# Gate's and up's products of a step issued chunk by chunk in turn instead of one whole product after the other

## The chip, the core and the metric

The kernel runs on one NeuronCore of a Trainium2 chip. The metric is the device time of one execution in microseconds (us). Three runs of the kernel before took 1248.95, 1249.93 and 1252.76 us; the median is 1249.93 us.

## What is computed

One block of a hybrid streaming encoder, for 1024 tokens of 1024 channels in float32: a Mamba-2 group and a stick-breaking attention group side by side, `out_proj`, and then the part that matters here, a SwiGLU channel mixer with 2816 hidden channels (`D_FF`):

```python
h = rms_norm(x, pre_ffn_gain[layer])
f = (jax.nn.silu(h @ w_gate[layer]) * (h @ w_up[layer])) @ w_down[layer]
x = x + rms_norm(f, post_ffn_gain[layer])
```

The changed code makes `h @ w_gate` and `h @ w_up`.

## The kernel before, in words

**How gate and up are tiled.** Gate and up are each made as the seven products of Winograd's form of Strassen's product. A quad `p` (0 to 10) is a pair of tiles of 128 hidden channels; the tokens are two blocks of 512, the 1024 input channels two halves. A *product* is [128 channels of f] x [512 tokens] summed over 512 input channels, so four chunks `k` of 128. Every operand is held as a high and a low part (`split`, lines 70 to 73: ScalarE makes the high part, VectorE the low part), and a chunk is three matmuls (`mm3`, lines 75 to 78: high x high, high x low, low x high). So a product is 12 matmuls of 128x128 by 128x512 into one PSUM bank (`product`, lines 887 to 891), all behind each other. Each matmul has its own load of weights (the left operand); the right operand is streamed.

**A step.** `quad(p, "g")` and `quad(p, "u")` (lines 896 to 928) are generators that give one product at each `next`. `step(p)` (lines 986 to 994) takes gate's next product and then up's: 12 matmuls of gate, 12 of up. Seven steps make a quad. Each of gate and up has four banks: `a` (products 0 and 1, with the right operands `B11` and `B21`), `b` (product 2, `T2`), `c` (products 3 and 5, `T3` and `T4`), `e` (products 4 and 6, `T1` and `B22`). The eight banks are taken from a ring of eight, so a bank comes back with the next quad. Product 1 adds to what product 0 left in bank `a`, and ScalarE copies bank `a` to `p1` between them (line 903); products 5 and 6 add to banks that VectorE read one step or more before.

**The left operands.** `left_gen` (lines 933 to 975) makes them, gate's and up's in turn; `pump(1 + LOOK)` ahead of each step keeps five steps' worth of pairs. There are ten pairs of places (`flhi`, `fllo`; tiles named `fhi`/`flo` in the pool `fw`), so a new pair waits until the step that used its place has been multiplied. The first two steps of quad 0 take theirs from `early_ops` (lines 1013 to 1022) instead, tiles `eo` in the pool `fwA`.

**Where the operands lie.** The pool `fw` is on the right side of SBUF, and so is `wo` (the operands of out_proj). `fwA` and `rpA`, `rpB` (the right operands `B11`, `B21`, `T2`, `T3` and `T1`, `T4`, `B22`) are on the left side. In out_proj (`out_mm`, lines 790 to 801) a bank gets 24 matmuls behind each other; the right operand is in `wo`, the left one (`yhl`) in `wo` too, but for positions 2 and 3, whose `yhl` takes the place of `T3` in `rpA` (line 764). The down product (`mms`, lines 1275 to 1280, and its loop from line 1286) has both operands on the right side, and gives three matmuls to each of four banks in turn.

**What sets the order.** The framework's planner orders the instructions of each engine before the run: in its own reckoning of time it takes, for an engine that is free, the earliest traced instruction whose inputs it reckons ready. The order in the program is the priority, not the order itself. On the chip each engine then runs its list in order.

**Round the change.** The first step of quad 0 stands before the products of out_proj's last position (line 1098), the second behind them (1116), quad 1's first two at lines 1124 and 1128 round `out_tail(7)`, which makes the last columns of `T2` and `T3`. From line 1230 on a loop goes through the rest: pump, step, gate (`gate`, lines 996 to 1004, makes a block of silu(gate) x up and stores it).

Of the kernel before, what the change touches and what calls it, by code (L numbers as in the profile page):

```python
# [13 lines left out]
PSUM = bass.MemoryType.PSUM  # L14
DRAM = bass.MemoryType.DRAM

P = 128
S = 1024
# [16 lines left out]
# what in_proj makes, in order; "ssd" from where on SSD's steps run beside the tiles  # L35
PLAN = ('qkv1', 'x0', 'x1', 'x2', 'x3', 'x4', 'x5', 'qkv2', 'x7', 'x6', 'ssd', 'qkv3', 'z0', 'z1', 'r0', 'z2', 'z3', 'wo', 'l1', 'o0')
# how far attention is where the other stream is 0, 1/8, .. 1 done
# [10 lines left out]
def tile_hybrid_block(  # L48
# [15 lines left out]
    """The rows of x and out run backwards in time (row s is token S-1-s), so that every  # L64
    running product over earlier tokens is a forward scan along the free axis."""
# [4 lines left out]
    def split(hi, lo, src):  # L70
        """hi + lo == src, hi and lo each exact in float32r."""
        A.copy(hi, src)  # L72
        V.tensor_tensor(lo, src, f32(hi), ALU.subtract)  # L73
# [6 lines left out]
    # ------------------------------------------------------------------ constants  # L80
# [20 lines left out]
    # TensorE's clock rises with use: products of ones while the first loads run  # L101
# [3 lines left out]
    # tri[s, l] = 1 where s >= l  # L105
    tri = const.tile([P, P], F32, name="tri")
    G.affine_select(tri, ones_f, [[-1, P]], ALU.is_ge, 0.0, base=0, channel_multiplier=1)
    # scan floor: 1 where the key is not strictly before the query, 0 elsewhere
# [3 lines left out]
    # column h is 1 on the 64 partitions of head h of a pair  # L112
# [11 lines left out]
    # DRAM scratch  # L124
# [5 lines left out]
    # means of squares and what they make 1 / rms: even heads, odd heads, SSD groups  # L130
# [8 lines left out]
    # ------------------------------------------------------------------ right side: x * gain and in_proj weights  # L139
# [4 lines left out]
    # the rows' 1 / rms scales columns here, so it is applied to what comes out of in_proj  # L144
# [13 lines left out]
    # sel16 sums the products of the two halves of w2  # L158
# [11 lines left out]
    # columns of w_in in the order of their use; each tile is loaded and split while the one before it  # L170
    # is multiplied
# [5 lines left out]
    def fetch_w(half=None):  # L177
        """The next column tile, or one half of it."""
        if cols:
            name, col = cols[0]  # L180
            w = w_tiles.setdefault(name, [])
            for dh in range(2) if half is None else (half,):
                w.append(load_w_half(col, name, dh))
            if len(w) == 2:
                cols.pop(0)
# [8 lines left out]
    # ------------------------------------------------------------------ pre-mix norm, first products  # L194
# [40 lines left out]
    # ------------------------------------------------------------------ left side: attention, conv and SSD work  # L235
# [20 lines left out]
    def qkv_tiles(j, st):  # L256
        """What takes q, k (each in its two parts) and v of a pair of heads out of PSUM, to DRAM."""
# [38 lines left out]
    # ------------------------------------------------------------------ dt, decays  # L296
    def dt_stage():
# [18 lines left out]
        # softplus(x) = max(x, 0) + log1p(exp(-|x|)), log1p(e) = 2 atanh(e / (2 + e))  # L316
# [43 lines left out]
        # attention's sigmoids, which need these, wait for the last exponential: ScalarE changes its table once  # L360
# [4 lines left out]
    # ------------------------------------------------------------------ conv tiles  # L365
# [38 lines left out]
    # ------------------------------------------------------------------ SSD  # L404
# [76 lines left out]
    def mean_sq(src, sel, rows, n, cnt, ps=None, start=True, stop=True):  # L481
        """Means of squares over channels, to the rows of ss_d."""
# [32 lines left out]
    # ------------------------------------------------------------------ stick-breaking attention  # L515
    CH = {128: [128], 256: [256], 384: [384], 512: [512], 640: [384, 256], 768: [512, 256], 896: [512, 384], 1024: [512, 512]}

    def prep_head(j, st, h):
        """Keys over both halves of the partitions, the query's high part beside its low part."""
# [29 lines left out]
    def weigh(head, qb):  # L549
        """A key k weighs sigmoid(z_k) * prod_{q < i < k} sigmoid(-z_i)."""  # L550
# [20 lines left out]
    def turn(ws, g, jj):  # L571
        """Weights of 256 queries and 256 keys, keys to the partitions, split."""
# [27 lines left out]
    def attention(st):  # L600
        """All heads, as one stream of small steps: products with the values lag the transposes,
        the next queries' weights run ahead of them."""
# [53 lines left out]
    def merge(ga, gb):  # L656
        """Interleave attention with the other stream, as PACE has it."""
# [47 lines left out]
    # ------------------------------------------------------------------ out_proj: the products  # L705
    # position p of a block of 128 tokens: from here on the last rows come first
# [14 lines left out]
    # the channels in the order of their use: attention's first, the SSD's second group last  # L721
    KO = (4, 5, 6, 7, 0, 1, 2, 3)

    def fetch_wo():
        """W_out's rows in the order of their use, and the places of their two parts."""
# [31 lines left out]
    def out_load(p, part):  # L757
        """A block of the mixed channels, scaled by their 1 / rms, split: all but the SSD's second
        group, that group, or all."""
# [89 lines left out]
    # ------------------------------------------------------------------ out_proj, post-mix norm, residual, pre-ffn norm  # L849
    # positions 0 .. 7 of a block of 128 tokens: from here on the last rows come first  # L850
# [3 lines left out]
    def row_rstd(ssq):  # L854
        """-2 (ssq / D + eps) ** -0.5 for [P, 2] partial sums; the gains it multiplies take in the -1 / 2."""
# [15 lines left out]
    # Gate and up as the seven products of Winograd's form of Strassen's product: blocks of 512  # L871
    # tokens, halves of d, and pairs of tiles of f. h2 is the right operand:
    #   [b11 b12; b21 b22], halves of d by halves of the tokens
# [13 lines left out]
    def product(ps, lop, rop, start):  # L887
        """ps = or += the product; a bank that was read goes on accumulating after that."""
        (ah, al), (bh, bl) = lop, rop
        for k in range(4):  # L890
            mm3(ps, ah[:, k, :], al[:, k, :], bh[:, k, :], bl[:, k, :], start and k == 0, k == 3, not start)

    gp = fw = None
    lops = []

    def quad(p, name):
        """The 2 x 2 blocks of W^T h from seven products. c11 is left in PSUM."""
# [3 lines left out]
        product(a, lops[x], B11, True)  # L901
# [3 lines left out]
        product(a, lops[x], B21, False)  # L905
        yield a
        b = bank("pb" + name)
        product(b, lops[x], T2, True)
# [4 lines left out]
        product(c, lops[x], T3, True)  # L913
# [4 lines left out]
        product(e, lops[x], T1, True)  # L918
        V.tensor_tensor(u3, e, u3, ALU.add)
        yield u3  # L920
        product(c, lops[x], T4, False)
# [3 lines left out]
        product(e, lops[x], B22, False)  # L925
# [7 lines left out]
    def left_gen():  # L933
        """The left operands in the order of their use, gate and up in turn."""
# [51 lines left out]
    def step(p):  # L986
        """The next product of gate's and of up's quad p."""
        if p not in quads:
            quads[p], done[p] = (quad(p, "g"), quad(p, "u")), 0
        cg, cu = [next(q) for q in quads[p]]  # L990
# [5 lines left out]
    def gate(t):  # L996
        """A block of a from gate's and up's."""
# [8 lines left out]
    # which block of a the products make  # L1006
    where = {1: (0, 0), 4: (1, 1), 5: (1, 0), 6: (0, 1)}

    with es_o:
# [3 lines left out]
        def early_ops():  # L1013
            """The left operands of the first two products."""
# [35 lines left out]
        def out_tail(sb, t):  # L1050
# [20 lines left out]
            # T3 = b22 - b12, T2 = T3 + b11, T1 = b12 - b11, T4 = b21 - T2: its product enters with that sign  # L1071
# [50 lines left out]
        # not the ring's next banks: those hold what waits for the last norm  # L1122
# [7 lines left out]
    # ------------------------------------------------------------------ gate and up  # L1130
# [241 lines left out]
```

## Time and profile before

| | |
|---|---|
| median of three runs | 1249.93 us |
| span of the profiled execution | 1249.6 us |
| TensorE busy (share of the span) | 1204.2 us (96%) |
| VectorE busy | 932.1 us (75%) |
| ScalarE busy | 587.7 us (47%) |
| mean granted TensorE clock | 0.989 |

The profile gives one execution. Its instruction rows cover the span, 1249.6 us from the first to the last instruction; the median of the separate runs is 0.3 us above it. A line such as `L76 PE MATMUL pag<-B11h,flhi` is line 76 of the kernel on TensorE: the product that writes gate's bank `a` (`pag`; `pau` is up's) from the right operand `B11`'s high part and the left operand's high part. PEld is the load of weights. `pd` are the down product's banks, `po` out_proj's. Matmuls overlap, so it is the distance from start to start that tells their pace, not the duration of one.

### The profile page before, as it was taken

What the parts mean: (1) busy time and instruction counts of PE and PEld (TensorE: products, weight loads), DVE (VectorE), ACT (ScalarE), POOL (GpSimd) and SP (SyncE); (2) the same over time, 40 slices, a digit from 0 to 9 for tenths busy, and PEclk for the clock granted to TensorE, in tenths of its full rate; (3) what the DMA queues carried; (4) which work ended last, traced back from release to release, by engine and by line L of the source; (5) the groups of instructions that cost most, each with busy time, mean ns of one, the idle gap of its engine ahead of it and who ended that gap; (6) DMA issues with size and microseconds to landing.
All of it is one profiled execution on the core that took longest, in us unless ns stands there. A gap on an engine that the chain in (4) does not pass through costs nothing.

```text
span 1249.6 us, 16320 instructions
## 1 busy us (share of the span) xinstructions
PE 1204.2 (96%) x5641; PEld 972.0 (78%) x5641; DVE 932.1 (75%) x1461; ACT 587.7 (47%) x1115; POOL 92.1 (7%) x232
## 2 busy tenths in 40 slices
PE   8998999999999998998799999999999999999997
PEld 7776778787887776787678888888888888888885
DVE  7478988778997887676897565566555558998777
ACT  7347655556655666444653332333233325444543
POOL 0041110010110100011200000000000000000000
PEclk9998999999999999999899999999999999999999
DMA  5693252445466326754872212312132198133336
GB/s 188 194 358 107 67 152 82 142 117 178 142 181 190 118 93 212 228 173 159 271 207 93 93 60 93 101 59 93 52 100 98 58 327 318 62 124 101 102 135 235
DMA packets 139882, 183.23 MB, mean 147 GB/s; under 512 B 10660, under 2 KB 94852, under 8 KB 139800
## 3 DMA queue, kind: packets, MB, share of 16 engines
q1 hardware_dynamic: 128544, 151.18, 38.3%
q0 software_dynamic: 7424, 25.17, 5.5%
q10 hardware_dynamic: 3832, 5.84, 1.3%
q8 instruction: 44, 0.72, 0.2%
q14 instruction: 38, 0.31, 0.1%
HBM read 132.23 MB, written 49.92 MB: 146 GB/s over the span
## 4 chain that ended last, share of the span: by engine, by line
PE 69%; DVE 14%; DMA 8%; issue 4%; ACT 4%; SPq 2%; DVEq 0%; ACTq 0%
PE pd L77 5%; PE pd L76 5%; PE pd L78 5%; DVE sn L567 3%; DMA Rb<-r_d 3%; PE o L590 2%; PE tp L578 2%; PE pj_x L76 2%; PE pj_x L78 2%; PE pcg L76 2%; PE pj_x L77 2%; PE pcu L76 2%; PE peg L76 2%; PE peu L76 2%; PE peu L77 2%
## 5 line engine op out<-in xcount | busy, mean ns | idle before, releaser
L72 ACT CAST flhi<-fraw 128x512 fp32r<-128x512 f32 x102 | 62.7, 622 | 174.1 <-PE pcg L77 37.0
L77 PE MATMUL pd<-folo,fohi 128*128 128x512 f32 x260 | 101.2, 389 | 0.0
L76 PE MATMUL pd<-fohi 128*128 128x512 f32 x260 | 101.2, 389 | 0.0
L78 PE MATMUL pd<-fohi,folo 128*128 128x512 f32 x260 | 101.1, 389 | 0.0
L567 DVE TENSOR_TENSOR_SCAN sn<-sn,smask 128x1024 f32<-128x1024 f32 (+3 forms) x64 | 87.4, 1366 | 17.7 <-ACT sn L563 17.7
L73 DVE TENSOR_TENSOR fllo<-fraw,flhi 128x512 fp32r<-128x512 f32 x102 | 69.6, 686 | 38.9 <-ACT flhi L72 38.5
L72 ACT CAST fohi<-rt 128x512 fp32r<-128x512 f32 x83 | 48.9, 618 | 51.2 <-PE pd L77 30.7
L563 ACT ACTIVATE sn<-zp,msc 128x512 f32<-128x512 f32 (+2 forms) x96 | 56.0, 585 | 34.3 <-PE zp L562 30.6
L582 ACT CAST wh<-tp 128x512 fp32r<-128x512 f32 (+1 forms) x80 | 42.7, 545 | 38.4 <-PE tp L578 37.9
L72 ACT CAST flhi<-fs 128x512 fp32r<-128x512 f32 x44 | 27.2, 622 | 70.4 <-PE peg L77 37.0
L73 DVE TENSOR_TENSOR folo<-rt,fohi 128x512 fp32r<-128x512 f32 x83 | 55.2, 694 | 6.4 <-ACT fohi L72 6.4
L583 DVE TENSOR_TENSOR wl<-tp,wh 128x512 fp32r<-128x512 f32 (+1 forms) x80 | 49.7, 628 | 10.8 <-ACT wh L582 10.3
L564 ACT ACTIVATE sp<-zp,msc 128x512 f32<-128x512 f32 (+2 forms) x96 | 55.8, 584 | 2.5 <-PE tp L578 2.5
L76 PEld LDWEIGHTS pd<-fohi 128*128 128x128 f32 x260 | 48.8, 188 | 10.3
L78 PEld LDWEIGHTS pd<-fohi,folo 128*128 128x128 f32 x260 | 48.8, 188 | 10.1
L77 PEld LDWEIGHTS pd<-folo,fohi 128*128 128x128 f32 x260 | 48.8, 188 | 10.1
L1004 POOL DMA_DIRECT2D a_d<-sg x44 | 23.7, 540 | 392.4 <-DVE sg L1003 392.4
L76 PE MATMUL pj_x<-hh,wh_x 128*128 128x512 f32 x128 | 52.5, 410 | 0.0
L578 PE MATMUL tp<-ident,sp 128*128 128x128 f32 x288 | 47.6, 276 | 5.0 <-DVE sp L568 4.5
L76 PE MATMUL po<-woh,yhl 128*128 128x512 f32 x128 | 51.0, 399 | 1.0 <-ACT yhl L72 1.0
L78 PE MATMUL po<-woh,yhl 128*128 128x512 f32 x128 | 51.0, 400 | 0.6 <-DVE yhl L73 0.5
L78 PE MATMUL pj_x<-hh,wl_x 128*128 128x512 f32 x128 | 51.1, 399 | 0.0
(422 smaller groups left out, 3479.4 us busy)
## 6 DMA issues: line engine op xcount, KB each, us to landing
ps<-a_d SPq DMA_DIRECT2D x55, 256.0 KB
fraw<-in_w_gate_dram SPq DMA_DIRECT2D x22, 512.0 KB
fraw<-in_w_up_dram SPq DMA_DIRECT2D x22, 512.0 KB
a_d<-sg POOLq DMA_DIRECT2D x44, 256.0 KB, 2.5
rt<-in_w_down_dram SPq DMA_DIRECT2D x33, 256.0 KB
rt<-a_d SPq DMA_DIRECT2D x22, 256.0 KB
ps<-in_w_down_dram SPq DMA_DIRECT2D x22, 256.0 KB
xt<-in_x_t_dram SPq DMA_DIRECT2D x8, 512.0 KB
```

What stands on the lines that cost most here:

```text
L72: A.copy(hi, src)
L73: V.tensor_tensor(lo, src, f32(hi), ALU.subtract)
L76: T.matmul(ps, lhsT=ah, rhs=bh, start=start, stop=False, skip_group_check=more)
L77: T.matmul(ps, lhsT=ah, rhs=bl, start=False, stop=False, skip_group_check=more)
L78: T.matmul(ps, lhsT=al, rhs=bh, start=False, stop=stop, skip_group_check=more)
L563: A.activation(sn[:, 1 + off : 1 + off + cw_], zp[:, 0:cw_], AF.Sigmoid, scale=rqn[:, qb : qb + 1])
L564: A.activation(sp[:, off : off + cw_], zp[:, 0:cw_], AF.Sigmoid, scale=rqp[:, qb : qb + 1])
L567: V.tensor_tensor_scan(sn[:, 1 : 1 + W], sn[:, 1 : 1 + W], smask[:, 0:W], 1.0, ALU.mult, ALU.max)
L578: T.transpose(tp[:, P * i : P * i + P], ws[a][:, co : co + P], ident)
L582: A.copy(wh[:, 0:n_], tp[:, 0:n_])
L583: V.tensor_tensor(wl[:, 0:n_], tp[:, 0:n_], f32(wh[:, 0:n_]), ALU.subtract)
L590: T.matmul(o[:, 0:cw_], lhsT=vv[:, k, h, :], rhs=wt[:, c0 : c0 + cw_], start=(first and k == kb + 1 and wt is wh), stop=(last and k == kb ...
```

## The change

`product` becomes a generator that stops after each of its first three chunks. `step` takes one chunk of gate's and one of up's in turn, until both are through. So a step is issued as 3 matmuls of gate, 3 of up, 3 of gate and so on; each product's evacuation stands directly behind its own last chunk, gate's ahead of up's last chunk. The matmuls, their operands, banks and flags are the same, and so are all other instructions. The rest of the diff takes out comments and docstrings.

```diff
     def product(ps, lop, rop, start):
         (ah, al), (bh, bl) = lop, rop
         for k in range(4):
             mm3(ps, ah[:, k, :], al[:, k, :], bh[:, k, :], bl[:, k, :], start and k == 0, k == 3, not start)
+            if k < 3:
+                yield MORE
 
     gp = fw = None
+    MORE = "more"
     lops = []
 
     def quad(p, name):
...
         a = bank("pa" + name)
-        product(a, lops[x], B11, True)
+        yield from product(a, lops[x], B11, True)
         p1 = e_tile(2 * x + p % 2, "p1" + name)
         A.copy(p1, a)
         yield
-        product(a, lops[x], B21, False)
+        yield from product(a, lops[x], B21, False)
         yield a
...
     def step(p):
         if p not in quads:
             quads[p], done[p] = (quad(p, "g"), quad(p, "u")), 0
-        cg, cu = [next(q) for q in quads[p]]
+        got = [MORE, MORE]
+        while any(g is MORE for g in got):
+            got = [next(q) if g is MORE else g for q, g in zip(quads[p], got)]
+        cg, cu = got
         del lops[:2]
```

The other five products of a quad are changed in the same way as the two shown.

## Rows read from the trace of the kernel before

**Rows 1.** The profile's page: busy time of each engine over the span; the granted TensorE clock in 40 slices of the span (tenths of full speed).

```profile
PE 1204.2 (96%) x5641; PEld 972.0 (78%) x5641; DVE 932.1 (75%) x1461; ACT 587.7 (47%) x1115; POOL 92.1 (7%) x232
...
PEclk9998999999999999999899999999999999999999
```

**Rows 2.** The chain of work that ended last, in order of time, round 639 us: start us, length us, what.

```profile
638.37 0.61 DVE u3g L915
...
639.12 0.47 PE pcg L76
```

**Rows 3.** Two stretches, gate's and up's stream from the chain's turn to TensorE on, and the down product: the stretch, its length, then busy us and instructions of each engine, the granted clock, the DMA share and GB/s.

```profile
639.12:1031.19 392.07, 392.07 (x1681) 315.45 (x1681) 238.81 (x374) 123.58 (x205) 22.12 (x41) 1.00 0.31 103
1031.19:1240.90 209.71, 209.55 (x924) 173.16 (x923) 180.65 (x308) 99.20 (x196) 0.54 (x1) 1.00 0.44 153
```

**Rows 4.** TensorE's matmuls in order of time, steps 0 and 1 of a quad in the middle of the stream: start us, duration us, line, out<-in.

```profile
795.99 0.40 PE L76 MATMUL pag<-B11h,flhi 128*128 128x512 f32 x1
...
798.32 0.40 PE L77 MATMUL pag<-B11l,flhi 128*128 128x512 f32 x1
798.56 0.39 PE L78 MATMUL pag<-B11h,fllo 128*128 128x512 f32 x1
798.79 0.40 PE L76 MATMUL pau<-B11h,flhi 128*128 128x512 f32 x1
...
801.59 0.40 PE L76 MATMUL pag<-B21h,flhi 128*128 128x512 f32 x1
```

**Rows 5.** The loads of weights at the same place.

```profile
798.56 0.19 PEld L76 LDWEIGHTS pau<-B11h,flhi 128*128 128x128 f32 x1
798.79 0.19 PEld L77 LDWEIGHTS pau<-B11l,flhi 128*128 128x128 f32 x1
```

**Rows 6.** Matmuls of the down product: 12 of them from the first row to the last.

```profile
1120.28 0.39 PE L76 MATMUL pd<-fohi 128*128 128x512 f32 x1
...
1123.00 0.39 PE L76 MATMUL pd<-doh 128*128 128x512 f32 x1
```

**Rows 7.** Matmuls of out_proj's position 6 (its `yhl` in `wo`), the 7th and the 22nd of the 24 that go to its first bank.

```profile
560.02 0.39 PE L76 MATMUL po<-woh,yhl 128*128 128x512 f32 x1
...
563.42 0.39 PE L76 MATMUL po<-woh,yhl 128*128 128x512 f32 x1
```

**Rows 8.** Matmuls of out_proj's position 3 (its `yhl` in `rpA`), the 4th and the 24th of the 24 that go to its first bank.

```profile
523.20 0.40 PE L76 MATMUL po<-woh,yhl 128*128 128x512 f32 x1
...
527.85 0.39 PE L78 MATMUL po<-woh,yhl 128*128 128x512 f32 x1
```

**Rows 9.** Matmuls of gate and up with the same right operands' pool: up's product 1 of quad 0, its first and last, with the left operand `eo`; then gate's product 0 of quad 1, its 2nd and 11th, with the left operand `fl`.

```profile
595.87 0.39 PE L76 MATMUL pau<-B21h,eo 128*128 128x512 f32 x1
...
598.37 0.39 PE L78 MATMUL pau<-B21h,eo 128*128 128x512 f32 x1
...
599.70 0.39 PE L77 MATMUL pag<-B11l,flhi 128*128 128x512 f32 x1
...
601.79 0.39 PE L77 MATMUL pag<-B11l,flhi 128*128 128x512 f32 x1
```

**Rows 10.** ScalarE at the place of rows 4: start us, duration us, line, out<-in, and idle time before with what ended it.

```profile
798.81 0.62 ACT L72 CAST flhi<-fraw 128x512 fp32r<-128x512 f32 x1 [2.18 <-PE pag L77]
799.34 0.58 ACT L903 COPY p1g<-pag 128x512 f32<-128x512 f32 x1
```

**Rows 11.** The instructions of the tile `pag`: the copy between products 0 and 1, with its count and its least, median and greatest duration (ns).

```profile
L903 ACT COPY p1g<-pag x11: 568/580/587, 583.5 to 995.3; 128x512 f32<-128x512 f32 x11
```

**Rows 12.** TensorE in quad 0, at the starts of steps 2 and 5.

```profile
617.84 0.50 PE L76 MATMUL pbg<-T2h,flhi 128*128 128x512 f32 x1 [3.26 <-ACT T2h L72]
619.07 0.79 PE L76 MATMUL pbu<-T2h,flhi 128*128 128x512 f32 x1 [0.72 <-ACT flhi L72]
619.66 0.63 PE L77 MATMUL pbg<-T2l,flhi 128*128 128x512 f32 x1
...
638.24 0.40 PE L78 MATMUL peu<-T1h,fllo 128*128 128x512 f32 x1
639.12 0.47 PE L76 MATMUL pcg<-T4h,flhi 128*128 128x512 f32 x1 [0.48 <-DVE u3g L915]
...
639.89 0.39 PE L76 MATMUL pcg<-T4h,flhi 128*128 128x512 f32 x1
```

**Rows 13.** ScalarE's cast that ends the wait at 617.84 us; VectorE's two reads of the banks `c` in quad 0.

```profile
617.20 0.59 ACT L72 CAST T2h<-pt 128x512 fp32r<-128x512 f32 x1 [1.66 <-DVE pt L1077]
...
638.29 0.69 DVE L915 TENSOR_TENSOR u3g<-pcg,p1g 128x512 f32<-128x512 f32 x1
...
639.49 0.69 DVE L915 TENSOR_TENSOR u3u<-pcu,p1u 128x512 f32<-128x512 f32 x1
```

**Rows 14.** The first step of quad 0: TensorE's first matmuls, and ScalarE's cast and VectorE's subtraction that make up's left operand.

```profile
574.33 0.77 PE L76 MATMUL pag<-B11h,eo 128*128 128x512 f32 x1 [3.75 <-DVE tm L1039]
574.89 0.63 PE L77 MATMUL pag<-B11l,eo 128*128 128x512 f32 x1
...
575.74 0.63 PE L76 MATMUL pag<-B11h,eo 128*128 128x512 f32 x1
...
576.80 0.60 ACT L72 CAST eo<-er 128x512 fp32r<-128x512 f32 x1
...
577.43 0.69 DVE L73 TENSOR_TENSOR eo<-er,eo 128x512 fp32r<-128x512 f32 x1 [0.35 <-ACT eo L72]
```

More of the change, by code (lines that the diff above doesn't have):

```diff
@@ L904, in quad @@
         yield
-        product(a, lops[x], B21, False)
+        yield from product(a, lops[x], B21, False)
         yield a
         b = bank("pb" + name)
-        product(b, lops[x], T2, True)
+        yield from product(b, lops[x], T2, True)
         V.tensor_tensor(p1, b, p1, ALU.add)
@@ L912, in quad @@
         c = bank("pc" + name)
-        product(c, lops[x], T3, True)
+        yield from product(c, lops[x], T3, True)
         u3 = e_tile(4 + x, "u3" + name)
@@ L917, in quad @@
         e = bank("pe" + name)
-        product(e, lops[x], T1, True)
+        yield from product(e, lops[x], T1, True)
         V.tensor_tensor(u3, e, u3, ALU.add)
         yield u3
-        product(c, lops[x], T4, False)
+        yield from product(c, lops[x], T4, False)
         c21 = tmp()
@@ L924, in quad @@
         yield c21
-        product(e, lops[x], B22, False)
+        yield from product(e, lops[x], B22, False)
         c12 = tmp()
```

## The prediction

> **What bounds the kernel now.** I read the page first: TensorE is busy 96% of the span, at the full granted clock but for two slices [rows 1]. But matmuls overlap, so a busy TensorE can still be issuing slower than it could. Next the chain of work that ended last: until 639 us other engines are on it, and with VectorE's read of gate's bank `c` it turns to TensorE [rows 2]. From there to the down product TensorE is busy without a break [rows 3]. So whatever the change does to TensorE's stream between 639 and 1031 us reaches the end one to one; what it does ahead of that has idle time to fall into.
>
> Next the pace. In gate's and up's stream 1680 matmuls take 392.07 us, 233.4 ns from start to start (the row counts 1681, one of them cut by the border). In the down product 924 take 209.71 us, 227.0 ns, and 12 of them without any disturbance 2.72 us, 226.7 ns [rows 3, 6]. The difference, 6.7 ns a matmul, is what the change could be after: 1680 x 6.7 = 11.2 us, 0.9%.
>
> **Is it the bank?** Two things differ between the streams: how often the bank changes (every 12 matmuls, every 3) and where the operands lie. The trace has cases that separate them.
> - Out_proj's position 6 gives 24 matmuls to one bank. From the 7th to the 22nd they take 3.40 us, 15 distances of 226.7 ns [rows 7]: the fast pace with the longest stay in a bank.
> - Position 3 runs the same lines with the same stay. Only its left operand lies in `rpA`, on the left, and its right one on the right: 20 distances take 4.65 us, 232.5 ns [rows 8].
> - Up's product 1 of quad 0 is the code that is changed, 12 matmuls in one bank. Its left operand `eo` and its right one `B21` both lie on the left: 11 distances in 2.50 us, 227.3 ns. Gate's product 0 a few us later has its left operand in `fw`, on the right: 9 distances in 2.09 us, 232.2 ns [rows 9].
> - The down product has both on the right, and is fast [rows 6].
>
> So 24, 12 and 3 matmuls to a bank all run at 227 ns where both operands are on one side, and 24 and 12 both at 232 to 233 where they are on two. The change of bank itself leaves no mark: `pag` to `pau` is 0.23 us like the distances beside it [rows 4]. The loads agree. Each load of weights starts with the matmul before it and lasts 0.19 us, and the next matmul starts 0.04 us behind its end [rows 4, 5]: a loop of load and matmul, with no bank in it. The change moves no operand. What the trace lacks is the fourth case, operands on two sides and a bank change every three: it is between 0 and -11.2 us, and I take 0, since three rows of four speak for the place and none for the bank.
>
> **The change part by part.**
> *Count.* No instruction is added or removed: 24 matmuls and 24 loads a step as before, the same casts, copies, DMAs. Generators cost nothing on the chip. No queue is moved past another.
>
> *The hand-over from product 0 to product 1* is what gets worse. Both use bank `a`, and ScalarE must have copied it in between. Now up's 12 matmuls (2.8 us) lie between gate's last one and its next into that bank; the copy takes 0.58 us [rows 11] and is hidden. Afterwards only three matmuls of up's lie there. Gate's last one starts at 798.56; its next would start 4 x 0.233 us later, at 799.49. But ScalarE first takes the cast for the pair that has just come free, and starts the copy at 799.34, to 799.92 [rows 10]; a matmul starts 0.05 us after the cast that it waits for (617.20 + 0.59 to 617.84) [rows 12, 13], so 799.97. That is 0.48 us of wait, and a stream that has stopped loses another 0.07 us (639.12 to 639.89 are three distances in 0.77 us instead of 0.70) [rows 12]: 0.55 us. If ScalarE takes up's cast ahead of up's copy as well, at its 0.53 us from start to start [rows 10], that copy ends at 800.98, and up's first matmul, due 0.77 us behind gate's, waits 0.29 + 0.07 us more: 0.9 us. Queued behind the wait is all of TensorE's stream. It comes once a quad; quad 0 has out_proj's last position in between, quad 1 has idle TensorE behind it (3.26 us [rows 12]), so it counts for quads 2 to 10: 9 x 0.55 = 5.0 us, 9 x 0.9 = 8.2 us at most.
>
> What can hide it is the planner. Where it reckons an input late, it takes the next matmul that is ready: at 619.07 it has put up's first matmul between gate's first and second, since gate's second needs `T2`'s low part [rows 12]. Product 2 needs neither bank `a` nor a new operand, so its first chunk can go into the gap; two matmuls are 0.47 us. Then nothing is lost but the rest of a matmul and perhaps the restart. Ends: 0 and 0.9 us a quad. I take 0.15 us (the 0.07 of the restart and a third of a matmul), as this planner has filled such a gap in this very stage: 9 x 0.15 = 1.4 us.
>
> The Trainium skill speaks against the change here: Perfetto Trace Analysis, Optimizing Tensor Performance, Matmuls, says that independent groups should rotate through banks so that the evacuation of one overlaps the next group's matmuls. The change rotates faster but leaves the evacuation of bank `a` less to overlap with; by that rule alone the unfilled price above holds. The copy that is hidden now agrees with it.
>
> *The other banks.* `c` is read between products 3 and 5, `e` between 4 and 6, with a step of 5.6 us (795.99 to 801.59 [rows 4]) between: nothing. Evacuations now come in pairs at a step's end, instead of 2.8 us apart; VectorE is busy 238.81 of 392.07 us [rows 3], and the next reader is a step away: nothing. One place is tight, quad 0's step 5. Gate's product waits there until 639.12 for VectorE; up's bank `c` is read from 639.49 to 640.18, and 0.14 us later (as for gate's) a matmul can start, at 640.32. Up's product comes a whole product behind gate's now; interleaved it is due at 639.89 [rows 12, 13]: 0.43 us, or 0 if gate's next chunk goes ahead. I take 0.2.
>
> *The places of left operands* come free for gate at the end of a step instead of its middle. They are refilled four steps ahead, 22 us: nothing.
>
> *Quad 0's first step.* Up's left operand is cast until 577.40 and has its low part at 578.12. It is needed behind gate's 12 matmuls now; interleaved, behind three, at 575.74 [rows 14]. Unfilled that is 1.7 us; gate's own chunks can fill it, and TensorE idles 3.26 us before 617.84 in any case [rows 12]. I take 0, and 1.7 as the end.
>
> *The pace after a stop.* With operands on two sides the pace has been 232.2 to 232.5 ns [rows 8, 9] and 233.4 [rows 3]; it went from the one to the other at the stop of 639 us. If new stops draw it anew, up to 1680 x 1.0 = 1.7 us come back. I take 0.
>
> Sum: 1.4 + 0.2 = 1.6 us on a span of 1249.6, 1251.2; the median of the runs is 0.3 above the span, so **1251.5 us**. Its own range is 1248 (pace 1.7 better, all filled) to 1254.5 (0.3 us a quad, 1.7 at the start).
>
> **The rivals.**
> *The bank sets the pace when the operands are on two sides.* For: the down product changes bank every three and is the fast one. Against: rows 7 to 9. Price 11.2 us: 1251.5 - 11.2 = 1240.3 us. 10%. A pace between the two: 1246, 2%.
>
> *The hand-over stays open.* The planner reckons the copy done in time, so it leaves the order as traced, and the chip waits once a quad. Place: the first matmul of product 1, quads 2 to 10. Price 5.0 us with 0.43 us at step 5 and some of the start: 1255.5; 8.2 us: 1259. It decides from 0.4 us a quad on (9 x 0.4 = 3.6 us). For: ScalarE's cast goes ahead of the copy now [rows 10]. Against: the filling at 619.07. 25%.
>
> *The clock falls.* If TensorE's short stops at each hand-over took the granted clock from 2.4 to 1.2 GHz, matmuls would start some 0.425 us apart as at 574.89 to 575.74 [rows 14], behind an idle 3.75 us; 12 such a quad cost 12 x 0.19 x 9 = 21 us: 1272. Against: the stop of 0.48 us at 639.12 left the pace at 0.23 us [rows 12], and the down product with its bank changes runs at a granted clock of 1.00 [rows 3]. 2%. The Trainium skill (TensorE: Matmul & The Clock Gate, A second HAM failure mode: psum-queue depth-cycling) tells of a kernel whose cycling through banks left such small gaps that the clock went up and down; by that page this rival would be likelier, but the down product's row is against it.
>
> *The change doesn't do what it says*: the planner puts whole products back behind each other. It takes them by the order of the program where all is ready, so only here and there: 3%, 1250.
>
> **How the numbers follow.** The forecast has 58%. This kernel's measurement tells 0.3% from no change, 3.75 us, so 1246.2 to 1253.7. Faster: the bank and the pace between, 12%. Slower: the open hand-over 25, the clock 2, and 4 of the forecast's 58: 31%. The same: 54 and the 3: 57%. The range leaves out the bank's 10%, the clock's 2 and the worse part of the open hand-over, some 6: 1247 to 1257.5.
>
> **What would show it.** Right: between 650 and 1030 us bank names change every three matmuls, distances stay at 232 to 234 ns, ScalarE's copy of `pag` starts 0.8 us after gate's last matmul, and some matmuls of `pbg` stand ahead of gate's product 1. The stretch from product 3 of quad 0 to the down product stays within 3 us of now. Wrong: distances at 227 ns (the bank), waits at gate's product 1 for line 903 of 0.4 us or more (the open hand-over), a granted clock under 1.00 in the stretch, or a wait of a place that I priced at nothing.

## The result, and the profile after

The kernel after takes 1255.14 us (median of 20 runs, 1250.81 to 1258.1), the kernel before 1250.35 us (20 runs on the same chip, 1246.5 to 1253.41). The ratio is 1.0036, with a 95% interval of 1.0026 to 1.0045: slower by 3.3 to 5.6 us. The profiled execution after has a span of 1253.9 us, 4.3 us more than that of before.

The page of the kernel after, busy time over the span and granted clock (the lines that answer to [rows 1]):

```profile
PE 1206.2 (96%) x5641; PEld 972.3 (78%) x5641; DVE 926.8 (74%) x1461; ACT 582.6 (46%) x1115; POOL 92.6 (7%) x232
...
PEclk9998999999999999999999999999999999999999
```

The page shows nothing: same instructions, same share. Where the 4.3 us arise is seen by cutting the execution at landmarks on TensorE. They are the first matmul of quad 0 (with `eo`), the last one of out_proj's position 7, the first with `T2`, the first with `T4`, the first of quad 0's last product (`B22`), the first of the down product and its last. Starts in us, from TensorE's rows in order of time:

| landmark | before | after | stretch before | stretch after | difference |
|---|---|---|---|---|---|
| first `eo` | 574.33 | 574.50 | | | 0.2 |
| position 7, last | 592.00 | 594.90 | 17.67 | 20.40 | 2.7 |
| `T2` | 617.84 | 620.68 | 25.84 | 25.78 | -0.1 |
| `T4` | 639.12 | 641.61 | 21.28 | 20.93 | -0.4 |
| `B22` | 644.79 | 648.81 | 5.67 | 7.20 | 1.5 |
| first `pd` | 1031.19 | 1035.49 | 386.40 | 386.68 | 0.3 |
| last `pd` | 1240.93 | 1245.27 | 209.74 | 209.78 | 0.0 |

**The first step of quad 0.** TensorE of the kernel after (the rows that answer to [rows 14], and the end of out_proj and the start of `T2`):

```profile
574.50 0.47 PE L76 MATMUL pag<-B11h,eo 128*128 128x512 f32 x1 [1.58 <-DVE tm L1045]
...
575.04 0.40 PE L78 MATMUL pag<-B11h,eo 128*128 128x512 f32 x1
577.63 0.50 PE L76 MATMUL pau<-B11h,eo 128*128 128x512 f32 x1 [2.19 <-ACT eo L72]
...
594.90 0.39 PE L78 MATMUL po<-woh,yhl 128*128 128x512 f32 x1
...
620.68 0.50 PE L76 MATMUL pbg<-T2h,flhi 128*128 128x512 f32 x1 [1.06 <-ACT T2h L72]
```

After three matmuls of gate TensorE stands 2.19 us and waits for the cast of up's left operand. Gate's next nine, whose operand is there, stand behind. ScalarE's rows show what the cast waited for:

```profile
575.64 0.63 ACT L1047 ACTIVATE tm<-x 128x512 f32<-128x512 f32 x1 [2.93 <-DVE x L1046]
...
576.98 0.60 ACT L72 CAST eo<-er 128x512 fp32r<-128x512 f32 x1
```

In ScalarE's list the cast stands behind the squares of position 5's norm (line 1047), and these wait 2.93 us for VectorE's `x`. Against the start of the step `eo` comes no later than before: its cast starts 2.48 us after gate's first matmul, 2.47 in [rows 14].

**The hand-over.** TensorE in quad 2 (the change's version of [rows 4]), the end of product 0 and the start of product 1:

```profile
686.93 0.40 PE L78 MATMUL pag<-B11h,fllo 128*128 128x512 f32 x1
687.16 0.39 PE L76 MATMUL pau<-B11h,flhi 128*128 128x512 f32 x1
687.39 0.39 PE L77 MATMUL pau<-B11l,flhi 128*128 128x512 f32 x1
687.62 0.39 PE L78 MATMUL pau<-B11h,fllo 128*128 128x512 f32 x1
687.85 0.39 PE L76 MATMUL pbg<-T2h,flhi 128*128 128x512 f32 x1
688.08 0.39 PE L77 MATMUL pbg<-T2l,flhi 128*128 128x512 f32 x1
688.34 0.51 PE L76 MATMUL pag<-B21h,flhi 128*128 128x512 f32 x1
688.68 0.39 PE L77 MATMUL pag<-B21l,flhi 128*128 128x512 f32 x1
```

and ScalarE at the same place, which answers to [rows 10]:

```profile
687.18 0.62 ACT L72 CAST flhi<-fraw 128x512 fp32r<-128x512 f32 x1 [3.73 <-PE pag L77]
687.71 0.58 ACT L906 COPY p1g<-pag 128x512 f32<-128x512 f32 x1
```

The copy starts 0.78 us after gate's last matmul, behind the cast, and ends at 688.29. Two matmuls of product 2 (`pbg`) fill the time. The two distances into and behind product 1's first matmul are 0.26 and 0.34 us instead of 0.23 each: 0.14 us.

**The stream** (which answers to the first of [rows 3]): the stretch, its length, then busy us and instructions of each engine, granted clock, DMA share, GB/s.

```profile
641.61:1035.49 393.88, 393.88 (x1680) 316.46 (x1681) 233.02 (x373) 118.16 (x204) 22.22 (x41) 1.00 0.31 103
```

It is 1.8 us longer than before, and 1.5 of that stand at its very start. TensorE behind `T4`, and the granted clock of that short stretch:

```profile
641.61 0.47 PE L76 MATMUL pcg<-T4h,flhi 128*128 128x512 f32 x1 [2.30 <-DVE u3g L918]
...
643.24 0.63 PE L76 MATMUL pcu<-T4h,flhi 128*128 128x512 f32 x1
643.67 0.63 PE L77 MATMUL pcu<-T4l,flhi 128*128 128x512 f32 x1
```

```profile
643.24:646.23 2.99, 2.99 (x9) 2.34 (x8) 2.99 (x7) 1.25 (x2) 0.00 (x0) 0.50 0.01 2
```

Before `T4` TensorE stood 2.30 us, where it stood 0.48 before [rows 12]; 1.6 us later the granted clock is 0.50 (the level of 1.2 GHz), and seven matmuls start 0.43 us apart instead of 0.23.

### The profile page after: what moved, and what is told of

It is laid out like the page before. It is cut to its first block, busy times and chain, and to the rows that moved or that the text cites. A ratio compares the mean times of both kernels' runs of the same rounds, so it can differ in the third digit from the quotient of the medians.

```text
span 1253.9 us, 16317 instructions
## 1 busy us (share of the span) xinstructions
PE 1206.2 (96%) x5641; PEld 972.3 (78%) x5641; DVE 926.8 (74%) x1461; ACT 582.6 (46%) x1115; POOL 92.6 (7%) x232
## 4 chain that ended last, share of the span: by engine, by line
PE 71%; DVE 13%; DMA 6%; ACT 4%; issue 4%; SPq 1%; DVEq 0%; ACTq 0%
PE pd L77 5%; PE pd L78 5%; PE pd L76 5%; DVE sn L567 3%; DMA Rb<-r_d 2%; PE o L590 2%; PE tp L578 2%; PE pcu L77 2%; PE pcg L76 2%; PE pcu L76 2%; PE pcg L78 2%; PE pcu L78 2%; PE pcg L77 2%; PE pj_x L76 2%; PE pj_x L78 2%
```

## The experiments

Two questions were open after this. Which of the 4.8 us (medians) does the first step make, which the hand-overs, and is the low clock behind `T4` part of the change? And what sets the pace of 233 ns, if not the bank? In the first two expectations theory A puts the loss at quad 0's first step and the rival B puts it at the hand-overs. In those on the padded kernel theory A holds both, with no part of the bank in the pace, and B is a price or a gain of the bank change itself. Each ratio is against runs of the kernel before on the same chip.

**The first step alone, taken out and put in.** A flag decides which steps go in turn:

```diff
-            if k < 3:
+            if k < 3 and turns[0]:
                 yield MORE
```

In the first run everything is as in the kernel after but quad 0's first step, which stays whole. In the second everything is as before, and only that step goes in turn.

> The changed kernel, but with the first step of quad 0 (ahead of out_proj's last position) issued as two whole products again; all other steps stay chunk by chunk. Theory A, the loss is made in that step: TensorE's wait of 2.19 us for up's left operand goes, quad 0's step 5 starts near 639.1 us instead of 641.6, the wait there is back at some 0.5 us, the clock does not fall behind it (1.5 us), and the time comes within 1.5 us of the kernel before (ratio 0.999 to 1.002). Rival B, the loss is the hand-over between products 0 and 1 of each quad: nothing of it comes back, ratio 1.003 to 1.005.

> The kernel before, with only the first step of quad 0 issued chunk by chunk; every other step as two whole products. Theory A: the whole loss is there, 3 to 5 us over the kernel before (ratio 1.0025 to 1.004), with the wait for up's left operand and the fallen clock in quad 0's step 5 in the trace. Rival B: same as the kernel before, ratio 0.999 to 1.001.

Measured: 1255.18 us and a ratio of 1.0040 (1.0024 to 1.0055) with the first step whole; 1253.57 us and 1.0025 (1.0015 to 1.0035) with only the first step in turn. The step alone costs some 3 us, with a wait of 2.2 us for `eo` in its trace. But with the step whole in the changed kernel the loss did not go away (1.0040, against 1.0036 for the whole change): theory A in its first form, that nearly all is made at the head, fell. The two don't add up to the whole either (4.5 + 2.9 = 7.4 us against 4.8), so something else moves between these kernels. The trace with the step whole accounts for 1.7 us more than before between the first `eo` and the first `pd`; another 2.1 us of its longer span lie ahead of `eo`. Their stretches from `T4` to the down product (same columns as above) show one thing that does. With the first step alone in turn:

```profile
642.41:1034.42 392.01, 392.00 (x1680) 317.76 (x1681) 238.29 (x374) 123.43 (x205) 22.22 (x41) 1.00 0.32 103
```

With the first step whole:

```profile
642.02:1034.95 392.93, 392.93 (x1681) 314.86 (x1681) 233.26 (x373) 118.06 (x204) 22.22 (x41) 1.00 0.31 104
```

The first of these has six or seven matmuls at 0.43 us in it, 1.5 us, and is still no longer than the 392.07 of before [rows 3]: away from them its pace is 232.4 ns, a quad 39.04 us; the second keeps 233.3 ns, 39.20 us a quad and 0.1 for each hand-over. In the kernel after, four of nine quads take 39.16 to 39.19 us and five 39.30 to 39.31. So the slow pace has two forms, up to 1.6 us apart over the stream, and a stop can change the form. A base without this was wanted, and it came out of the second question.

**What sets the pace.** The prediction's rows told the bank from the place of the operands, but not what in the place it is. In the compiled program the pools with gate's and up's right operands begin at bytes 34400 and 99936 of a partition, 1632 modulo 2048. The pool with their left operands begins at 163808, which is 2016: a difference of 384. `eo`, which is fast with `B21` [rows 9], lies at 1632 like it. The left operands of out_proj's position 3 in `rpA`, slow, lie 384 from `wo`. Side and difference agree in all rows of before. A pad ahead of `fwA` shifts the left side, without changing sides or order:

```diff
+    padp = ctx.enter_context(tc.tile_pool(reuse_waits="tile", name="padp", bufs=1, side="left"))
+    padp.tile([P, 32], F32, name="pad")
     fwA = ctx.enter_context(tc.tile_pool(reuse_waits="tile", name="fwA", bufs=1, side="left"))
```

32 floats are 128 bytes (a difference of 256); 96 are 384 bytes (0; there `ssq` of the down product was moved to another pool, to make room); 64 are 256 bytes (128); 16 are 64 bytes (320).

> The same with 128 bytes instead of 384, so that the two sides' tiles stand 256 bytes apart modulo 512. If the pace hangs on the two addresses modulo 256 or less, it is 227 ns and the time 1239 to 1241 us; if modulo 512 or more, or not on addresses at all, 233 ns and the time of the kernel before.

> The kernel before, whole products, with 384 bytes a partition left empty in front of the left side's pools of gate and up (and the down product's sums of squares put into a tile that is free by then, to make room). Products, order and banks as before, only the address of the left side's tiles moves: in the compiled program the left side's tiles start at 1632 bytes modulo 2048 and the right side's at 2016, and now both at 2016. Theory P1, the pace hangs on where the two operands' addresses stand to each other: gate's and up's stream goes from 233.4 to some 227 ns a matmul, 10 to 11 us less, 1239 to 1241 us (ratio 0.991 to 0.992). Theory P2, it is the distance or the side: pace and time as before (ratio 0.999 to 1.001). Rival P3, the stay of 12 matmuls in a bank makes the slow pace: as before too.

> The kernel before with a pad of 256 bytes: the right operands of gate and up then lie 128 bytes from the left ones modulo 2048, instead of 384 without a pad (233 ns), 256 with 128 (226.7 ns) and 0 with 384 (226.7 ns). If the pace hangs on the difference modulo 256, it is 232 to 234 ns here; if only the one difference of 384 is slow, 226.7 ns.

> The kernel before with a pad of 64 bytes: a difference of 320 modulo 2048, 64 modulo 256. If only differences that are whole multiples of 256 are fast, 230 to 234 ns; if the slow ones are those at 128 modulo 256, 226.7 ns.

The stretches from `T4` to the down product (columns as above), 1680 matmuls each, with 128 bytes, 384, 256 and 64:

```profile
640.28:1021.20 380.92, 380.92 (x1681) 315.39 (x1682) 238.42 (x374) 123.53 (x205) 22.14 (x41) 1.00 0.33 105
```

```profile
642.10:1023.03 380.93, 380.93 (x1681) 315.39 (x1682) 238.37 (x374) 123.55 (x205) 22.22 (x41) 1.00 0.33 106
```

```profile
637.78:1028.26 390.48, 390.48 (x1681) 316.92 (x1681) 238.27 (x374) 123.37 (x205) 22.12 (x41) 1.00 0.32 104
```

```profile
641.20:1033.27 392.07, 392.07 (x1680) 315.92 (x1681) 238.46 (x374) 123.56 (x205) 22.12 (x41) 1.00 0.33 104
```

380.92 / 1680 is 226.7 ns, the pace of the down product; 390.48 / 1680 is 232.4 and 392.07 / 1680 is 233.4, the two forms of the slow pace. So the difference of the addresses decides: 0 and 256 are fast, 320, 128 and 384 slow, as if it had to be a multiple of 256. It is the difference and not the left side's address alone, since `eo` with `B21` is fast at 1632 [rows 9].

Out_proj's positions 2 and 3, whose `yhl` the pads shift against `wo`, are a second test in the same traces, with the left operand at the lower address. The 4th and the 24th matmul of position 3, as in [rows 8], with 128 bytes and with 64:

```profile
525.08 0.39 PE L76 MATMUL po<-woh,yhl 128*128 128x512 f32 x1
...
529.62 0.39 PE L78 MATMUL po<-woh,yhl 128*128 128x512 f32 x1
```

```profile
525.78 0.39 PE L76 MATMUL po<-woh,yhl 128*128 128x512 f32 x1
...
530.36 0.39 PE L78 MATMUL po<-woh,yhl 128*128 128x512 f32 x1
```

With 128 bytes the 20 distances take 4.54 us, 227 ns instead of 232.5. With 64 they take 4.58 us, 229 ns: a third pace, with the left operand 320 below the right one instead of 320 above it. So fast and slow are not all there is, and the exact rule has these few points behind it and no more.

The medians: 1241.7 us with 128 bytes, ratio 0.9938 (0.9918 to 0.9958), and 1243.8 with 384, 0.9948 (0.9931 to 0.9965); the kernels with 256 and 64 were timed once each, 1248.4 and 1253.27. The gain in the stream is 392.07 - 380.92 = 11.1 us, the very 11.2 us that the prediction named as what the change could be after. Of these the medians show 9.0 and 6.9 us, so both times lie above the 1239 to 1241 us that were expected; in the traces part of the rest is lost ahead of the stream, which starts at 640.28 and 642.10 us instead of 639.12.

**The change's parts on the padded base.** With 128 bytes the pace has one form, so the same parts were run there. The flag is now a condition on the quad `p` and the step `i`:

```diff
-            if k < 3:
+            if k < 3 and in_turn(*now):
                 yield MORE
...
+    in_turn = lambda p, i: p > 1 and i < 2
```

This is the one for the hand-overs of quads 2 to 10. `i > 1` takes the other products alone, `p == 0 and i == 0` the first step, `p + i > 0` all but that; the whole change has no condition.

> The kernel before with the pad of 128 bytes once more, beside the three others on one chip: 1240.5 to 1243, pace 226.7 ns, quads of 38.08 us.

> On the padded kernel before, only products 0 and 1 of quads 2 to 10 go in turn: the nine hand-overs from product 0 to product 1 alone. Theory A: 9 x 0.11 = 1.0 us above the padded kernel before, with quad 0's head as in that kernel; 1242 to 1243.5, and quads of 38.2 us instead of 38.08. If the planner left them open it would be 9 x 0.5, 4.5 us.

> On the padded kernel before, only products 2 to 6 of every quad go in turn, products 0 and 1 stay whole. Theory A: the same as the padded kernel before within 0.5 us but for quad 0's T4, where TensorE waits for VectorE; if the longer wait there and the clock behind it come from the turns in products 2 to 6, this run shows them (up to 2 us), if from the late first step, it doesn't. Theory B: quads differ from 38.08 us.

> The whole change, with a pad of 128 bytes ahead of the pool fwA, which in the kernel before took the matmuls of gate and up from 232.4 to 226.7 ns. Theory A (the change costs at quad 0's head and at nine hand-overs, and the pace is a matter of the operands' relative addresses alone): the pace in the stream is 226.7 ns here too; the nine hand-overs cost 0.11 us each, 1.0 us, the first step up to 2.7 us, the fall of the clock behind T4 some 1.5 us more, so 3 to 5 us above the padded kernel before, 1244.5 to 1247. Theory B (a bank change every three matmuls has a price or a gain of its own, hidden so far under the slow pace): distances away from 226.7 ns, by 1 ns for 1.7 us.

> On the kernel before with the pad of 128 bytes (1241.5 us), only the first step of quad 0 goes in turn. Theory A (that step's wait for up's left operand reaches the end): up's first matmul waits some 2.2 us, the stretch from the first matmul to the last of out_proj's position 7 is 20.4 instead of 17.8 us, and 1.5 to 3 us of it stand at the end: 1243 to 1244.5. Rival (the idle time ahead of T2 and T4 takes it in, as the prediction had it): 1241 to 1242.

> On the same padded kernel, every step goes in turn but the first of quad 0. Theory A: the nine hand-overs of quads 2 to 10, 2.0 us as measured alone, and quad 1's hand-over, where the copy of gate's bank ends a wait of 0.9 us of which a part reaches the end: 1243.5 to 1244.5, and with the first step's loss it makes up the 5.8 us of the whole change on this base. Rival (the turns disturb each other, so that the parts don't add up): 1245.5 or more.

The first four ran beside each other on one chip, the last two on another, where the kernel before took 1249.46 us instead of 1250.37. The last two columns are from TensorE's rows of the profiled execution; whole spans are not set beside each other, because the first `eo` already starts anywhere from 573.55 to 578.38 us in these executions, although the order of each engine's instructions up to there is the same in all of them:

| in turn | median us | ratio to before (95%) | `eo` to `T4` | `T4` to `pd` |
|---|---|---|---|---|
| nothing | 1241.49 | 0.9928 (0.9914 to 0.9942) | 64.96 | 382.46 |
| products 2 to 6 | 1241.63 | 0.9935 (0.9922 to 0.9949) | 65.74 | 380.92 |
| products 0, 1 of quads 2 to 10 | 1243.5 | 0.9953 (0.9937 to 0.9968) | 66.06 | 382.62 |
| quad 0's first step | 1244.6 | 0.9959 (0.9945 to 0.9973) | 67.97 | 382.50 |
| all but that step | 1244.75 | 0.9963 (0.9949 to 0.9976) | 64.91 | 382.56 |
| everything | 1247.31 | 0.9969 (0.9954 to 0.9984) | 68.36 | 384.16 |

*The bank.* With products 2 to 6 in turn the stream takes what it takes with nothing in turn, to the last digit of the pad's first run:

```profile
642.25:1023.17 380.92, 380.92 (x1681) 315.39 (x1681) 231.74 (x373) 119.96 (x204) 22.14 (x41) 1.00 0.32 105
```

A bank change every three matmuls neither costs nor gives anything; theory B is out.

*The hand-overs.* Nine of them, with nothing else:

```profile
644.44:1027.06 382.62, 382.62 (x1680) 314.72 (x1681) 237.78 (x374) 121.59 (x205) 22.14 (x41) 1.00 0.32 105
```

382.62 - 380.92 = 1.7 us, 0.19 each (each of the nine quads takes 38.27 us instead of 38.08); the median gives 2.0. Expected were 0.11 each, 1.0. In the whole change on the pad the same place reads:

```profile
689.83 0.39 PE L78 MATMUL pag<-B11h,fllo 128*128 128x512 f32 x1
...
690.73 0.39 PE L76 MATMUL pbg<-T2h,flhi 128*128 128x512 f32 x1
690.96 0.39 PE L77 MATMUL pbg<-T2l,flhi 128*128 128x512 f32 x1
691.24 0.50 PE L76 MATMUL pag<-B21h,flhi 128*128 128x512 f32 x1
691.58 0.40 PE L77 MATMUL pag<-B21l,flhi 128*128 128x512 f32 x1
```

0.28 and 0.34 us instead of 0.227 each: filled with the same two matmuls, and a little dearer than on the slow pace: from gate's last matmul to product 1's first it is 1.41 us on both, while the six distances in it are shorter here.

*The first step.* TensorE with only that step in turn:

```profile
577.24 0.63 PE L78 MATMUL pag<-B11h,eo 128*128 128x512 f32 x1
579.39 0.80 PE L76 MATMUL pau<-B11h,eo 128*128 128x512 f32 x1 [1.52 <-ACT eo L72]
```

The distance is 2.15 us instead of 0.43 (it was still at the low clock), and the stretch from `eo` to `T4` 67.97. Over all kernels this stretch is 63.7 to 66.1 us in the ten executions with the step whole, 65.2 in the mean, and 67.1 to 68.9 in the four with it in turn, 68.1 in the mean: 2.8 us, with no overlap. The median gives 3.1 us raw, and 3.9 when each is set against the kernel before on its own chip (0.0031 of the time). That is at or a little above the upper end of theory A's 1.5 to 3; the rival that idle time takes it in is out.

*The clock behind `T4`.* With nothing in turn, the repeated pad shows it too:

```profile
638.87 0.76 PE L76 MATMUL pcg<-T4h,flhi 128*128 128x512 f32 x1 [2.10 <-DVE u3g L917]
```

```profile
639.43:642.40 2.97, 2.97 (x9) 2.34 (x8) 2.97 (x6) 1.25 (x2) 0.00 (x0) 0.53 0.13 41
```

Its stream is 382.46 where the other run of the same kernel has 380.92: 1.5 us. And with all but the first step in turn TensorE waits 2.46 us there, and the clock stays:

```profile
640.58 0.47 PE L76 MATMUL pcg<-T4h,flhi 128*128 128x512 f32 x1 [2.46 <-DVE u3g L922]
```

```profile
640.58:646.10 5.52, 5.52 (x24) 4.58 (x25) 5.52 (x10) 1.41 (x3) 0.00 (x0) 1.00 0.29 91
```

So the fall at `T4` does not need the change. But it stands in all four traces in which the first step goes in turn (behind waits of 1.96 to 2.30 us) and in one of the ten in which that step is whole (waits of 0.48 to 2.46 us). With one trace a kernel that does not show a cause, and it does not exclude one: the 1.5 us may be part of what the first step costs, as theory A had it.

*The sum.* By medians it is 3.1 for the first step, 2.0 for the hand-overs and 0.1 for the rest: 5.2 us, against 5.8 for the whole change (theory A had 3 to 5). By the ratios it is 3.9, 3.1 and 0.9: 7.9 us against 5.1. The interval of each ratio is some 1.8 us to either side, so the parts fit the whole no closer than that. "All but the first step" costs 3.3 us by medians and 4.4 by the ratios, where 2.1 were due by medians; so taking the first step out of the whole change gives back 2.6 us by medians and 0.8 by the ratios, and on the kernel without a pad nothing. On both bases the first step alone and all but it make more together than the whole (8.1 us against 4.5 without a pad and 8.3 against 5.1 with it, by the ratios). Whether the one loss hides part of the other, or this is spread, is not shown. The trace of all but the first step has one more wait, at quad 1's product 1:

```profile
608.38 0.50 PE L76 MATMUL pag<-B21h,flhi 128*128 128x512 f32 x1 [2.26 <-ACT p1g L910]
```

but its stretch from `eo` to `T4` is 64.91, among the shortest. The first experiment's has a wait of 1.46 us there and a stretch of 65.61. Whether that wait reaches the end in other executions, or the 1.2 us too much are just the spread of runs that reach from 1241.56 to 1247.78, stays open; a run with quad 1's hand-over alone was not made. What the first experiment's 4.5 us have beyond the hand-overs stays open too.

No version with the turns beat the one with nothing in turn. The fastest kernel here is the one of before with 128 bytes of pad: 1241.5 and 1241.7 us on two chips, some 0.7% under the kernel before, over 1% under the kernel after.

## Why the prediction was right or wrong

The time, 1255.14 us, is within the range, but the likeliest case (no difference, 1251.5) did not come: the change is slower by 0.4%, which had 31 in 100, and lies beyond the forecast's own 1248 to 1254.5. That the time lies next to the 1255.5 us of the open hand-over is chance, since the loss is not made there.

**What bounds the kernel, and the bank.** Right: TensorE's stream is without a break from `T4` on, and the bank has no part in its pace; the 10% and 2% for it went to nothing. "One to one" is not borne out in full: the pads took 11.1 us out of the stream and 6.9 to 9.0 off the medians. The reason was only half right. "Operands on two sides" fits all rows of before, but it was a stand-in for the difference of the addresses: the pads leave both operands on their sides, and two of four make the stream fast. In [rows 7 to 9] side and difference change together, so they could not tell them apart.

**The hand-over.** Right in mechanism and size: cast ahead of copy, copy 0.78 us behind gate's last matmul, two matmuls of product 2 in the gap, 0.14 us at the slow pace against 0.15 forecast (0.19 at the fast one). The rival of the open hand-over, 25%, did not come: in quads 2 to 10 no more than 0.14 us (0.19 on the padded base) is lost there. Its sign, a wait of 0.4 us or more for line 903's copy (906 in the kernel after), shows in quad 1 alone, 0.91 us there; the prediction had left that quad out, and no trace shows that the wait reaches `T4`. What the Trainium skill says of it (Perfetto Trace Analysis, Optimizing Tensor Performance, Matmuls: rotating banks lets evacuation overlap with matmuls) fits: the trace shows the overlap restored by the planner, with two matmuls of another bank.

**Quad 0's first step.** This is the step that failed: "gate's own chunks can fill it, and TensorE idles 3.26 us before 617.84 in any case [rows 12]. I take 0, and 1.7 as the end." Both halves were wrong. The planner filled the hand-overs but not this gap: it put up's three matmuls next, and on the chip the cast of `eo` stood behind ScalarE work that waited for VectorE. Why it reckoned the cast early enough is not in the trace. And the idle time at 617.84 is no cushion for it, because it belongs to a chain that starts behind the delayed matmuls. The products of position 7 stand behind this step on TensorE, its norm behind them, and `T2` behind the norm. The chain of work that ended last in the kernel after goes this way (start us, length us, what; as [rows 2]):

```profile
577.07 0.52 ACT eo L72
577.63 0.50 PE pau L76
...
595.07 0.23 PE po L78
...
595.77 1.08 ACT hT L1068 x2
596.85 1.17 ACT tm L1039 x4
...
608.65 3.46 DMA b<-h_d
...
620.05 0.59 ACT T2h L72
620.68 0.50 PE pbg L76
```

From the late cast it goes through TensorE's matmuls to position 7's `po`, the squares of its norm (line 1039), and on to `T2`. In the kernel before, the chain passed this place beside TensorE, through VectorE and a load of left operands that landed at 595.72:

```profile
591.08 4.64 DMA head<-in_w_gate_dram
```

With 64 and with 256 bytes of pad, that step whole, the chain goes through `po` as well, so the two ways were about equally long.

From position 7's last matmul to `T2` it is 25.78 us after and 25.84 before, and over all fourteen traces 24.9 to 26.9: with the first step in turn (25.8 to 26.9) it is not shorter, so the idle time in it did not take the delay in. The size was short as well: in the four traces TensorE waits 1.5 to 2.2 us, and the stretch is 2.8 us longer in the mean, against 1.7.

**Quad 0's step 5.** 0.2 us were taken for up's wait at `T4`. There was none: gate's second chunk went ahead of up's first matmul, which the prediction had as its lower end. Gate's own wait there was 2.30 us instead of 0.48; it runs from 0.48 to 2.46 over the kernels with that first step whole, and is 1.96 to 2.30 in the four with it in turn. The run with products 2 to 6 in turn costs 0.1 us by medians, so the interleaving of this step is not what makes it longer.

**The clock.** Priced at the hand-overs, 2%. The granted clock did not fall there (1.00 over the stream). What the Trainium skill tells of a clock that goes up and down with small gaps in the cycling through banks (TensorE: Matmul & The Clock Gate, A second HAM failure mode: psum-queue depth-cycling) has no sign at the nine hand-overs. The clock did fall at `T4`, at a price of 1.5 us that the prediction did not have; there it fell behind a wait for VectorE.

**The pace after a stop.** Right in kind and in its bound: the two forms, 39.04 and 39.20 us a quad, can change at stops. Four of nine quads had the better one, 4 x 0.16 = 0.6 us back, which is why nine hand-overs of 0.10 to 0.14 us show as only 0.3 us in the stretch from `B22` to `pd`.

**The sum again.** Forecast: 1.4 for the hand-overs, 0.2 at step 5, 0 for the first step. Measured on the padded base, by medians: 2.0 (1.7 by the trace), 0.1 for all of products 2 to 6, 3.1. The largest error is the first step. It is not shown to be the only one: without it the kernels still lose 4.5 us (no pad) and 3.3 us (pad), more than the hand-overs explain.

## What to carry to other kernels

Idle time covers a delay only if what ends it does not itself wait for the delayed work: before a wait is priced at nothing, follow the next idle stretch back to its source and see whether the delayed instruction stands on that path. When work of two streams is interleaved, look at the first use of each operand: the finer the interleaving, the sooner the second stream's operand is due, and it is the place where it is made last that pays. And where the same matmul has two paces in one trace, compare the addresses of its operands and not just their pools: here a pad of 128 bytes brought 9 us, and no order of the products that was tried brought any.

## What the runs showed of the hardware that was not expected

The distance of back-to-back matmuls (128x128 by 128x512, each with its own load of weights) went with the difference of the two operands' SBUF addresses, left minus right, modulo 256: 226.7 ns at 0, 232.4 to 233.4 ns at 64 and 128, 229 ns at 192. The slow pace at 128 has two forms, 232.4 and 233.3 ns, and the stream can change from one to the other at a stop. And the clock fell to 0.50 behind waits of 1.96 to 2.30 us at the same place where it stayed at 1.00 behind ones of 2.07 and 2.46 us: the length of that wait alone does not decide it.
